# An S5, GLA and differential-attention trunk on one core: phase pieces of the first S5 layer, scaled sides of the second and attention's first split in another order

## The chip, the cores and the metric

The kernel runs on 1 core of one Trainium2 chip. The metric is device time in microseconds (us), the median of several executions. Engines: TensorE (PE) multiplies matrices, with its weight loads (PEld) beside it; VectorE (DVE) and ScalarE (ACT) work element by element; GpSimd (POOL) clears tiles and issues DMAs; SyncE (SP) issues most DMAs. Each engine works through its own instructions in order and waits on semaphores for the others.

## The reference

A batch of one, 512 positions, 1024 features, four layers: S5, gated linear attention (GLA), differential attention, S5. Each layer is a mixer and a SwiGLU network, each behind an RMS norm and added to its input. What matters here is the S5 mixer: 64 groups of 16 features have 64 complex states each, with a decay, a rotation per step, an input matrix and an output matrix:

```
p_ang = li * dt * j
p_re = p_mag * jnp.cos(p_ang)
p_im = p_mag * jnp.sin(p_ang)
...
y = jnp.einsum('bcgp,ghp->bcgh', s_re, cr) - jnp.einsum('bcgp,ghp->bcgh', s_im, ci)
...
y = y + d_skip.astype(f32) * h.astype(f32)
z = jax.nn.gelu(y).astype(h.dtype)
a, b = jnp.split(z @ w_glu, 2, axis=-1)
return a * jax.nn.sigmoid(b)
```

The attention projects to q, k and v, turns a quarter of each head by its position, and takes for each of 8 heads the difference of two softmaxes, `a = p[:, :, 0] - lam * p[:, :, 1]`, times v.

## The kernel before, in words

All is float32. A matrix product at full width is made of parts: each operand is split into a high part (a cast to the PE's float32 format) and a low part (the operand less its high part), and three products are added (`mm3`, L376, L377, L378). For weights the high part is cast by ACT (`high`, L348, tile whl) and the low part subtracted by DVE (`low_now`, L356); weights come through three staging tiles (wst) and lie in five whl tiles. PSUM has four banks for sums (acc), two for V (s) and two for turned tiles and small outputs (tp).

**An S5 layer** is a pipe over eight blocks of 128 features (`s5_pipe`, L1341). For block kk: its input is transposed (`up`, L1366, PE) and copied to a tile "room" by ACT (L1379), or in the second S5 layer for the first four blocks multiplied by the norm's factor on DVE (L1375, Rt); `products` gives V on PE (L1387); `states` turns V by cosines and sines on DVE (L1392 to L1397); two scans with the decays run along time on DVE (L1401); four `turn`s turn back on DVE (L1414, L1410) and leave prods; `outputs` adds y on PE (L1421 with the block's map from a DMA to scr, L1423 with prods) and takes its gelu on ACT (L1425); `turned` transposes it (zp, L1438, PE) and casts it to zT (L1439, ACT); `rest` subtracts its low part (L1443, DVE); `glu` multiplies two steps later with the gate's weights.

A step of the loop (ten of them) issues, in order: states(kk), outputs(kk-1), up(kk+2), turned(kk-1), products(kk+1), the scans and turns of kk, rest(kk-1), glu(kk-2). Between these stand hooks, named by their place ("behind states", "operators", "ahead of zp", "behind products", "behind scans", "beside"). In this pipe all five engines keep the order in which the code issues (`hand_all`): a step's place in the code is its place in each engine's row.

The first S5 layer has to make its cosines and sines itself, in the hooks. Each block has four pieces (`s5_phases_first`): **rough** (two products on PE, L1012 and L1013, then two roundings on ACT, L1014 and L1016, to tile turnsr), **angle** (three products on PE, L1020 to L1022, the second of which needs turnsr), **clip** (one DVE instruction, L1025, which reads the angle and writes cs), **sines** (three ACT instructions: Abs L1028, Sin L1029, Sin L1030). states of a block needs its sines. Beside these the hooks build, for every two blocks, the input matrices (X, L1052 to L1054 and L1077 on DVE; transposed as xps, L1188, PE; copied as inm, L1211, ACT), the output matrices (Q; transposed as cps, L1098, PE; copied, L1119, ACT; L1052 to L1054, DVE), and the map within a block: rps (L1154, PE), its two copies rsb (L1164, DVE; L1168, ACT), a DMA to memory (rd, L1170) and eight DMAs back to scr (L1179). The decays r are copied by ACT (L1038). Sin and gelu use different tables of ACT; where one follows the other an ACT_TABLE_LOAD stands between.

In the second S5 layer these matrices come from memory; its first four blocks are transposed ahead of the norm (`up_first`), and their multiply by Rt is what `up` issues in steps 0 and 1 for blocks 2 and 3.

**The attention** (L2090) fixes only PE's order by hand; the other engines' rows are set by a scheduler, which `issue_after` can bind to stand behind a given instruction. A projection is 32 units of three products, drawn by `run(units, n)`; the evacuation of a projection to q or k is L2152 (ACT), L2157 to L2163 (DVE), a transposition L2168 and a copy L2169 (ACT); that of v is L2174 (ACT). `prepare(j)` splits the queries and keys of head j: tile hl, high part on ACT (L2188), low part on DVE (L2189), then DMAs of POOL's queue to qs and ks. The code around the change:

```
units = project(0, 2)
run(units, 8)
rest()
prepare(0)
run(units)
```

Of the kernel before, what the change touches and what calls it, by code (L numbers as in the profile page):

```python
# [268 lines left out]
class Trunk:  # L269
# [1071 lines left out]
    def s5_pipe(self, L, hu, zT, natural, room, get, before=None, hooks=None, steps=None, left=None):  # L1341
# [114 lines left out]
        if hooks:  # L1456
            hook = lambda name, kk: hooks[name](kk) if name in hooks else None
            self.hand_all()
            if left:
                for kk in range(4):  # L1460
                    up_first(kk)
            before(up, products)
            for kk in range(10):
                if kk % 2 == 0 and kk:
                    hls[kk // 2 - 1] = self.high(stage[kk // 2 - 1], 2, 512)
                hook("first", kk)
                if kk < 8:
                    states(kk)
                if kk == 7:
                    rest(5)  # L1470
                if kk % 2 == 0 and kk:
                    self.low(hls[kk // 2 - 1], stage[kk // 2 - 1])
                hook("behind states", kk)
                if 1 <= kk < 9:
                    outputs(kk - 1)
                hook("operators", kk)
                if kk + 2 < 8:
                    up(kk + 2)
                hook("ahead of zp", kk)
                if 1 <= kk < 9:  # L1480
                    turned(kk - 1)
                if kk == 8:
                    glu(6)
                if kk + 1 < 8:
                    products(kk + 1)
                hook("behind products", kk)
                if kk < 8:
                    scan(kk, 0)
                    scan(kk, 1)
                    hook("behind scans", kk)  # L1490
                    for k in range(4):
                        turn(kk, k)
                hook("beside", kk)
                if 1 <= kk < 9 and kk != 6:
                    rest(kk - 1)
                if kk % 2 == 0 and kk < 8:
                    stage[kk // 2] = self.staged(self.wb_src(wg, kk, D), 2, 512)
                if kk >= 2 and kk != 8:
                    glu(kk - 2)
                hook("last", kk)  # L1500
            self.hand()
            return accs
# [33 lines left out]
    def s5_first(self, ctx):  # L1536
# [5 lines left out]
        with self.tc.tile_pool(name="s5_0", bufs=1) as p:  # L1542
# [92 lines left out]
                raw[2] = self.s5_loads(p, 0, 16, 8, 2)  # L1635

            def first(kk):
                if kk == 1:
                    phases((5, "angle"))
                if kk == 2:  # L1640
                    raw[3] = self.s5_loads(p, 0, 24, 8, 2)
                if 1 <= kk < 7:
                    decays(kk + 1)

            def behind_states(kk):
                if kk == 0:
                    phases((1, "clip"))
                    self.s5_map(0, 0, 8, rv[0], rs, mops[0])

            def operators(kk):  # L1650
                if kk in (2, 4, 6):
                    h = kk // 2
                    rv[h] = self.s5_rows(8, bp, Q[h][0])
                    if h > 1:
                        self.s5_map(0, 8 * h, 8, rv[h], rs, mops[h % 2])
                if 1 <= kk < 7:
                    ins(kk + 1)
# [5 lines left out]
            def behind_products(kk):  # L1663
                if kk == 0:
                    phases((3, "angle"), (4, "rough"))
                if kk == 1:
                    phases((6, "rough"), (7, "rough"), (6, "angle"))
                if kk == 2:
                    phases((7, "angle"))
                if kk == 3:  # L1670
                    phases((4, "sines"), (5, "sines"), (6, "sines"), (7, "sines"))
                if kk % 2 == 0 and 2 <= kk < 7:
                    out_pads(kk + 1)

            def behind_scans(kk):
                if kk == 0:
                    phases((2, "clip"), (2, "sines"), (4, "angle"), (5, "rough"))
                if kk == 1:
                    phases((4, "clip"), (5, "clip"))
                if kk == 2:  # L1680
                    self.s5_map(0, 8, 8, rv[1], rs, mops[1])
                    phases((6, "clip"))

            def beside(kk):
# [8 lines left out]
                    self.s5_b_pads(bp, X[h + 1][0])  # L1693
                if kk % 2 == 0 and kk < 6:
                    new_q(h + 1)
                if kk == 0:
                    phases((3, "clip"), (3, "sines"))
                if kk % 2 and kk < 7:
                    Q[h + 1][2]()
                    Q[h + 1][3]()  # L1700
                    out_pads(kk + 1)

            rv = {}
            hooks = {
                "first": first, "operators": operators, "behind states": behind_states, "ahead of zp": ahead_of_zp,
                "behind products": behind_products, "behind scans": behind_scans, "beside": beside,
            }
            accs = self.s5_pipe(0, hu, zT, True, room, get, before, hooks)
# [377 lines left out]
    def diff(self, l, left, after):  # L2086
# [4 lines left out]
        with self.tc.tile_pool(name="diff", bufs=1) as p:  # L2091
# [185 lines left out]
            units = project(0, 0)  # L2277
            run(units)
            tables()
            units = project(0, 1)  # L2280
            run(units)
            units = project(0, 2)
            run(units, 8)
            rest()
            prepare(0)
            run(units)

            def projections():
# [146 lines left out]
```

## Time and profile before

| what | us |
|---|---|
| median of three executions | 2316.88 |
| lowest, highest | 2314.95, 2317.75 |
| the profiled execution | 2316.13 |
| its span | 2314.4 |

A profile holds one execution. A row of the timeline gives the start, the length, engine, line, operation, what is written and read, the shape and, in brackets, how long the engine was idle ahead of it and who released it. Rows of one engine overlap a little: what an instruction costs its engine is the distance from its start to the next one's. A product on PE is a pipelined matmul, so its row is longer than that distance. A row of the waits adds such idle times by who waited for whom. A window gives the busy time of each engine in a stretch, and "PEclk", the share of full speed at which PE's clock ran there. The first S5 layer's pipe runs from about 38 to 165 us, the attention's first half to 1256, the second S5 layer's pipe from about 1804.

### The profile page before, as it was taken

Reading aid. Unit: us, or ns where it says so; the run is one execution under the profiler, and the core shown is the slowest. Engines: PE = TensorE matmul, PEld = TensorE weight load, DVE = VectorE, ACT = ScalarE, POOL = GpSimd, SP = SyncE. Lnnn points to the kernel's source line nnn. Section 1 sums busy time; section 2 is a strip of 40 time slices with the busy share of each in tenths; the row PEclk is TensorE's granted clock in tenths of the full one; section 3 lists DMA queues with packets and bytes.
Section 4 is the critical chain, followed back from the end, with each engine's and each line's share of the span. In section 5 each row is a group of like instructions: output and inputs, shape, how many; then the busy total and the mean of one; then the engine's idle time right before and its main releaser. Section 6 shows DMA issues by size and latency. Waiting matters only on the chain. (4 is left out here: it accounts for less than half of the span.)

```text
span 2314.4 us, 37179 instructions
## 1 busy us (share of the span) xinstructions
PE 2219.4 (96%) x14847; PEld 1970.1 (85%) x14847; DVE 1593.2 (69%) x2461; ACT 1108.2 (48%) x1769; POOL 284.6 (12%) x394
## 2 busy tenths in 40 slices
PE   5899999999999999999999999999999899999997
PEld 3788979898877799898988787899999788989996
DVE  8784977786624578777745675976766965957674
ACT  5533645454453355555535675654534224635342
POOL 1000140522000010100002131110000100101000
PEclk9999999999999999999999999999999899999999
DMA  4156567663422457665237365886641555766521
GB/s 86 39 146 172 131 173 183 164 179 100 124 71 73 137 140 190 170 177 164 92 124 156 90 152 136 223 210 146 163 103 46 140 153 150 201 157 162 159 80 64
DMA packets 293927, 319.91 MB, mean 138 GB/s; under 512 B 70077, under 2 KB 233177, under 8 KB 293498
## 3 DMA queue, kind: packets, MB, share of 16 engines
q1 hardware_dynamic: 231130, 235.79, 33.6%
q0 software_dynamic: 62624, 81.75, 18.9%
q8 instruction: 117, 1.92, 0.3%
q14 instruction: 56, 0.46, 0.1%
HBM read 285.62 MB, written 16.65 MB: 131 GB/s over the span
## 5 line engine op out<-in xcount | busy, mean ns | idle before, releaser
L356 DVE TENSOR_TENSOR whl<-wst,whl 128x1024 fp32r<-128x1024 f32 x272 | 331.1, 1222 | 264.5 <-ACT whl L348 263.4
L348 ACT CAST whl<-wst 128x1024 fp32r<-128x1024 f32 x272 | 284.3, 1050 | 336.9 <-PE acc L378 232.8
L543 PE MATMUL a<-side,whl 128*128 128x256 f32 x3168 | 382.4, 277 | 6.1 <-DVE whl L356 6.0
L543 PEld LDWEIGHTS a<-side,whl 128*128 128x128 f32 x3168 | 369.9, 188 | 7.8 <-DVE whl L356 6.7
L376 PE MATMUL acc<-whl,act 128*128 128x512 f32 x704 | 278.0, 395 | 2.6 <-DVE g L588 2.6
L377 PE MATMUL acc<-whl,act 128*128 128x512 f32 x704 | 274.9, 390 | 0.0
L378 PE MATMUL acc<-whl,act 128*128 128x512 f32 x704 | 274.7, 390 | 0.0
L543 PE MATMUL c<-side,whl 128*128 128x256 f32 x2112 | 256.2, 278 | 7.2 <-DVE whl L356 7.2
L543 PEld LDWEIGHTS c<-side,whl 128*128 128x128 f32 x2112 | 248.4, 189 | 8.2 <-DVE whl L356 8.2
L356 DVE TENSOR_TENSOR whl<-slot,whl 128x1024 fp32r<-128x1024 f32 x105 | 127.8, 1222 | 66.0 <-ACT whl L348 65.9
L376 PEld LDWEIGHTS acc<-whl,act 128*128 128x128 f32 x704 | 132.1, 188 | 31.9 <-DVE g L588 3.0
L378 PEld LDWEIGHTS acc<-whl,act 128*128 128x128 f32 x704 | 132.2, 188 | 27.9
L377 PEld LDWEIGHTS acc<-whl,act 128*128 128x128 f32 x704 | 132.2, 188 | 25.9 <-issue 0.2
L348 ACT CAST whl<-slot 128x1024 fp32r<-128x1024 f32 x105 | 110.0, 1053 | 74.0 <-PE acc L378 28.2
L376 PE MATMUL acc<-whl,hT 128*128 128x512 f32 x352 | 142.8, 406 | 2.1 <-DVE ro L2160 1.5
L377 PE MATMUL acc<-whl,hT 128*128 128x512 f32 x352 | 138.0, 392 | 0.9 <-DVE whl L356 0.9
L378 PE MATMUL acc<-whl,hT 128*128 128x512 f32 x352 | 138.1, 392 | 0.0
L543 PE MATMUL a<-sides,whl 128*128 128x256 f32 x1056 | 133.9, 283 | 1.2 <-DVE x L526 1.2
L543 PE MATMUL d<-sides,whl 128*128 128x256 f32 x1056 | 133.4, 282 | 1.3 <-ACT whl L348 1.3
L543 PEld LDWEIGHTS a<-sides,whl 128*128 128x128 f32 x1056 | 129.4, 191 | 2.3 <-issue 1.6
L543 PEld LDWEIGHTS d<-sides,whl 128*128 128x128 f32 x1056 | 128.8, 191 | 1.9 <-ACT whl L348 1.9
L680 ACT CAST act<-r 128x512 fp32r<-128x512 f32 (+1 forms) x110 | 66.2, 644 | 105.1 <-DVE r L661 86.1
(449 smaller groups left out, 3901.1 us busy)
## 6 DMA issues: line engine op xcount, KB each, us to landing
wst<-in_ffn_w_gate_up_dram SPq DMA_DIRECT2D x88, 512.0 KB, 4.5
wst<-in_ffn_w_down_dram SPq DMA_DIRECT2D x88, 512.0 KB, 4.4
slot<-in_ffn_w_gate_up_dram SPq DMA_DIRECT2D x69, 512.0 KB, 5.8
wst<-in_ffn_w_gate_up_dram POOLq DMA_DIRECT2D x44, 512.0 KB, 6.1
halves<-in_ffn_w_gate_up_dram SPq DMA_DIRECT2D x42, 512.0 KB, 5.5
wst<-in_s_w_glu_dram SPq DMA_DIRECT2D x32, 512.0 KB, 4.9
wst<-in_gla_w_in_dram SPq DMA_DIRECT2D x24, 512.0 KB, 3.6
wst<-in_diff_w_qkv_dram SPq DMA_DIRECT2D x24, 512.0 KB, 4.0
```

The costliest lines, as they stand in the source:

```text
L348: self.last["high"] = self.nc.scalar.copy(hl[:, 0], w[:])
L356: self.last["low"] = self.nc.vector.tensor_tensor(hl[:, 1], w[:], hl[:, 0].bitcast(F32), op=ALU.subtract)
L376: mm(out, lh, rh, start=first, stop=False)
L377: mm(out, lh, rl, start=False, stop=False)
L378: self.last["mm"] = mm(out, ll, rh, start=False, stop=last)
L543: mm(o, hl[:, x, k, c], side[:, y, k], start=first and not (j or k or n), stop=k == 3 and n == 2, skip_group_check=True,)
L680: self.last["act high"] = nc.scalar.copy(dst[:, 0, j], src[:, j])
```

## The change

Three edits, all of order; no instruction is added but two loads of ACT's tables.

First S5 layer: the angles of blocks 4 and 5 move from ahead of y(0) to the hook "operators" of step 1, behind y(0); those of blocks 6 and 7 to that of step 2, behind y(1). The clip and sines of block 3 move up behind states(1), the clips of blocks 4 and 5 down behind Q's DVE work in step 1. The sines of blocks 4 to 7, so far one row of twelve ACT instructions in step 3, go to a new hook "behind zp": blocks 4 and 5 in step 3, blocks 6 and 7 in step 4.

Second S5 layer: the multiplies of blocks 2 and 3 by Rt are issued behind the turns of steps 0 and 1 instead of ahead of V.

Attention: nine more units of the value projection are issued ahead of prepare(0), which is bound behind the last weight split issued by then.

```diff
--- before.py
+++ after.py
@@ -1474,11 +1474,13 @@
                 if 1 <= kk < 9:
                     outputs(kk - 1)
                 hook("operators", kk)
-                if kk + 2 < 8:
+                late = left and kk + 2 < 4
+                if kk + 2 < 8 and not late:
                     up(kk + 2)
                 hook("ahead of zp", kk)
                 if 1 <= kk < 9:
                     turned(kk - 1)
+                hook("behind zp", kk)
                 if kk == 8:
                     glu(6)
                 if kk + 1 < 8:
@@ -1490,6 +1492,8 @@
                     hook("behind scans", kk)
                     for k in range(4):
                         turn(kk, k)
+                if late:
+                    up(kk + 2)
                 hook("beside", kk)
                 if 1 <= kk < 9 and kk != 6:
                     rest(kk - 1)
@@ -1635,8 +1639,6 @@
                 raw[2] = self.s5_loads(p, 0, 16, 8, 2)
 
             def first(kk):
-                if kk == 1:
-                    phases((5, "angle"))
                 if kk == 2:
                     raw[3] = self.s5_loads(p, 0, 24, 8, 2)
                 if 1 <= kk < 7:
@@ -1646,8 +1648,14 @@
                 if kk == 0:
                     phases((1, "clip"))
                     self.s5_map(0, 0, 8, rv[0], rs, mops[0])
+                if kk == 1:
+                    phases((3, "clip"), (3, "sines"))
 
             def operators(kk):
+                if kk == 1:
+                    phases((4, "angle"), (5, "angle"))
+                if kk == 2:
+                    phases((6, "angle"), (7, "angle"))
                 if kk in (2, 4, 6):
                     h = kk // 2
                     rv[h] = self.s5_rows(8, bp, Q[h][0])
@@ -1664,19 +1672,17 @@
                 if kk == 0:
                     phases((3, "angle"), (4, "rough"))
                 if kk == 1:
-                    phases((6, "rough"), (7, "rough"), (6, "angle"))
-                if kk == 2:
-                    phases((7, "angle"))
-                if kk == 3:
-                    phases((4, "sines"), (5, "sines"), (6, "sines"), (7, "sines"))
+                    phases((6, "rough"), (7, "rough"))
                 if kk % 2 == 0 and 2 <= kk < 7:
                     out_pads(kk + 1)
 
+            def behind_zp(kk):
+                if kk in (3, 4):
+                    phases((2 * kk - 2, "sines"), (2 * kk - 1, "sines"))
+
             def behind_scans(kk):
                 if kk == 0:
-                    phases((2, "clip"), (2, "sines"), (4, "angle"), (5, "rough"))
-                if kk == 1:
-                    phases((4, "clip"), (5, "clip"))
+                    phases((2, "clip"), (2, "sines"), (5, "rough"))
                 if kk == 2:
                     self.s5_map(0, 8, 8, rv[1], rs, mops[1])
                     phases((6, "clip"))
@@ -1693,16 +1699,16 @@
                     self.s5_b_pads(bp, X[h + 1][0])
                 if kk % 2 == 0 and kk < 6:
                     new_q(h + 1)
-                if kk == 0:
-                    phases((3, "clip"), (3, "sines"))
                 if kk % 2 and kk < 7:
                     Q[h + 1][2]()
                     Q[h + 1][3]()
                     out_pads(kk + 1)
+                if kk == 1:
+                    phases((4, "clip"), (5, "clip"))
 
             rv = {}
             hooks = {
-                "first": first, "operators": operators, "behind states": behind_states, "ahead of zp": ahead_of_zp,
+                "first": first, "operators": operators, "behind states": behind_states, "ahead of zp": ahead_of_zp, "behind zp": behind_zp,
                 "behind products": behind_products, "behind scans": behind_scans, "beside": beside,
             }
             accs = self.s5_pipe(0, hu, zT, True, room, get, before, hooks)
@@ -2282,7 +2288,9 @@
             units = project(0, 2)
             run(units, 8)
             rest()
-            prepare(0)
+            run(units, 9)
+            with self.tc.issue_after(self.last["high"].ins), self.tc.issue_after(self.last["low"].ins):
+                prepare(0)
             run(units)
 
             def projections():
```

PE in the first S5 layer, around y(0) (the rows L1421 and L1423) and ahead of it (- before, + changed; "angle" is a block's three products, cps the transposition for Q, xps the one for inm):

```order
 L1013 MATMUL rough<-counts,frow 128x512
-L1020 MATMUL angle<-counts,frow 128x512
-L1021 MATMUL angle<-turnsr,nident 128x512
-L1022 MATMUL angle<-counts,frow 128x512
 L1012 MATMUL rough<-counts,frow 128x512
 L1013 MATMUL rough<-counts,frow 128x512
 L1098 MATMUL cps<-ident,craw 64x128 x8
-L1020 MATMUL angle<-counts,frow 128x512
-L1021 MATMUL angle<-turnsr,nident 128x512
-L1022 MATMUL angle<-counts,frow 128x512
 L1421 MATMUL y<-scr_97,room_348 128x128
 L1423 MATMUL y<-scr_97,prods 128x128 x4
```

The six angle products of blocks 4 and 5 now stand behind y(0), ahead of xps. In the same way those of blocks 6 and 7 stand behind y(1), ahead of rps, where block 6's stood ahead of y(1) and block 7's behind V(3).

ACT in the first S5 layer, steps 3 and 4 (cs are the sines' tiles, z and gain the gelu's, Q the copies of cps):

```order
-L1028 ACTIVATE cs_351<-cs_351 128x512
-L1029 ACTIVATE cs_351<-cs_351 128x512
-L1030 ACTIVATE cs_351<-cs_351,halfpi 128x512
-L1028 ACTIVATE cs_351<-cs_351 128x512
-L1029 ACTIVATE cs_351<-cs_351 128x512
-L1030 ACTIVATE cs_351<-cs_351,halfpi 128x512
-L348 CAST whl<-wst 128x1024
-L1038 COPY r_1035<-s5r_127 128x512
+L348 CAST whl<-wst 128x1024
+L1038 COPY r_1029<-s5r_127 128x512
 L1425 ACT_TABLE_LOAD
 L1425 ACTIVATE z_349<-y 128x8x4x16
```

```order
 L1439 CAST zT<-zp 128x4x128
+L1028 ACTIVATE cs_351<-cs_351 128x512
+L1029 ACT_TABLE_LOAD
+L1029 ACTIVATE cs_351<-cs_351 128x512
+L1030 ACTIVATE cs_351<-cs_351,halfpi 128x512
+L1028 ACTIVATE cs_351<-cs_351 128x512
+L1029 ACTIVATE cs_351<-cs_351 128x512
+L1030 ACTIVATE cs_351<-cs_351,halfpi 128x512
 L1119 ACTIVATE Q<-cps 64x8x16 x4
 L1038 COPY r_1199<-s5r_127 128x512
+L1425 ACT_TABLE_LOAD
 L1425 ACTIVATE gain<-y 128x8x4x16
```

Two blocks' sines leave the place ahead of gelu(3) and stand, with a load of Sin's table ahead and one of gelu's behind, between zT(3) and gelu(4), ahead of the Q copies.

ACT in the attention, around the first split (hl), first before, then changed (qtm and qk are a projection's evacuation, vall the values'):

```order
L2152 ACTIVATE qtm<-acc,rcol 128x512 x4
L348 CAST whl<-wst 128x1024
L2169 COPY qk<-qTp 128x4x128 x4
L2152 ACTIVATE qtm<-acc,rcol 128x512 x4
L2169 COPY qk<-qTp 128x4x128 x4
L2188 CAST hl<-qk 128x1024
L348 CAST whl<-wst 128x1024 x5
L2188 CAST hl<-qk 128x1024 x2
L2174 ACTIVATE vall<-acc,rcol 128x512 x4
```

```order
L2158 ACTIVATE qtm<-acc,rcol 128x512 x4
L348 CAST whl<-wst 128x1024
L2175 COPY qk<-qTp 128x4x128 x4
L348 CAST whl<-wst 128x1024 x2
L2158 ACTIVATE qtm<-acc,rcol 128x512 x4
L2175 COPY qk<-qTp 128x4x128 x4
L2194 CAST hl<-qk 128x1024
L348 CAST whl<-wst 128x1024 x3
L2194 CAST hl<-qk 128x1024 x2
L2180 ACTIVATE vall<-acc,rcol 128x512 x4
```

Two of the five weight casts behind hl now stand ahead of the last qtm copies; DVE's two subtractions move likewise. The order of PE is unchanged there, and so are the rows of POOL and SP everywhere.

## The prediction

> **What bounds the kernel now.** The page comes first: which engine fills the span.
>
> ```profile
> PE 2219.4 (96%) x14847; PEld 1970.1 (85%) x14847; DVE 1593.2 (69%) x2461; ACT 1108.2 (48%) x1769; POOL 284.6 (12%) x394
> ```
>
> TensorE (PE) is busy in 2219.4 of 2314.4 us, so at most 95 us are idle, and an edit that computes nothing less can only close idle time or make PE run faster. The three edits lie in three short stretches, so each is read there: waits, timeline, windows. The first S5 layer (38 to 165 us) comes first. VectorE's (DVE's) waits in its first half are "engine, line, for whom: total, times, longest":
>
> ```profile
> DVE cs L1025 <- PE angle L1022: 5.8, 3, 4.1
> DVE zT L1443 <- ACT zT L1439: 3.9, 1, 3.9
> DVE rsb L1164 <- PE rps L1154: 2.2, 1, 2.2
> DVE whl L356 <- ACT whl L348: 0.4, 1, 0.4
> ```
>
> These 12.3 us are DVE's idle time from 50 to 88. The windows show what comes behind, and the clock (columns: stretch, length, then busy and count of PE, PEld, DVE, ACT, POOL; PEclk, DMA share, GB/s):
>
> ```profile
> 56.00:59.40 3.40, 3.40 (x14) 1.76 (x11) 2.26 (x4) 2.82 (x8) 0.00 (x0) 0.50 0.02 5
> 73.10:76.40 3.30, 3.30 (x15) 3.06 (x16) 2.90 (x5) 2.18 (x3) 0.11 (x1) 0.53 0.02 5
> 88.00:155.00 67.00, 58.95 (x583) 52.76 (x581) 66.52 (x110) 30.46 (x51) 6.69 (x16) 0.97 0.31 69
> ```
>
> From 88 to 155 DVE works 66.52 of 67.00 us. What it gains before 88 it can keep, and nothing but DVE limits it there. The first two rows show PE at half clock around y(0) and y(1), with PE wholly busy.
>
> **First S5, the path of PE.** The timeline of PE (start, length, then the instruction, and the idle time before it):
>
> ```profile
> 50.45 0.39 PE L1012 MATMUL rough<-counts,frow 12*128 12x512 f32 x1
> 50.92 0.38 PE L1020 MATMUL angle<-counts,frow 12*128 12x512 f32 x1
> ...
> 56.63 0.79 PE L1020 MATMUL angle<-counts,frow 12*128 12x512 f32 x1
> 58.80 0.80 PE L1421 MATMUL y<-scr,room 128*128 128x128 f32 x2
> ...
> 65.49 1.15 PE L1188 MATMUL xps<-ident,X 64*64 64x64 f32 x32
> ...
> 71.32 0.38 PE L1020 MATMUL angle<-counts,frow 12*128 12x512 f32 x1
> ...
> 73.39 0.80 PE L1421 MATMUL y<-scr,room 128*128 128x128 f32 x2
> ...
> 79.64 0.69 PE L1154 MATMUL rps<-Q,bpad 128*32 128x64 f32 x32
> ...
> 86.52 0.50 PE L1020 MATMUL angle<-counts,frow 12*128 12x512 f32 x1
> ...
> 87.81 1.09 PE L1098 MATMUL cps<-ident,craw 128*64 128x128 f32 x16
> ...
> 92.58 0.46 PE L1421 MATMUL y<-scr,room 128*128 128x128 f32 x2 [0.71 <-DMA scr<-rd]
> ...
> 97.21 1.15 PE L1188 MATMUL xps<-ident,X 64*64 64x64 f32 x32
> ...
> 109.23 0.69 PE L1154 MATMUL rps<-Q,bpad 128*32 128x64 f32 x32
> 113.23 1.15 PE L1188 MATMUL xps<-ident,X 64*64 64x64 f32 x32 [3.31 <-ACT z L1425]
> ```
>
> Prices: an angle product is 1.29 warm (86.52 to 87.81) and 2.17 cold (56.63 to 58.80); y is 4.63 warm (92.58 to 97.21), while y(0) took 6.69 and y(1) 6.25. A rough product takes 0.47 (50.45 to 50.92).
>
> Angles 4 and 5 leave the way to y(0), with angle 4's wait for its turns. Behind rough(4) (to 50.92) stand rough(5), 0.47, and the C transposes (cps), 1.09 warm: y(0) may start at 52.5 instead of 58.80. It also needs block 0's map, whose last DMAs are these:
>
> ```profile
> 47.12 2.35 POOL L1179 DMA_DIRECT2D scr<-rd  x4 [2.12 <-DMA rd<-rsb]
> ...
> scr<-rd POOLq DMA_DIRECT2D x4, 32.0 KB, 2.1
> ```
>
> Issued by 49.5 and landing 2.1 later, the map is there at 51.6. y(0)'s length isn't shown by any row, since the clock may be either; between 4.63 and 6.69 I take the middle, 5.66, because the angles' small products, which filled the time right ahead of y(0) and waited there, leave, while V and the roughs stay. So y(0) ends at 58.1, angles 4 and 5 (2 x 1.29) at 60.7, and xps(2) starts there: 4.8 ahead. ScalarE (ACT) now has sines(3) behind states(1) and a table load behind them, ahead of gelu(0); if these come late, the angles' 2.6 on PE cover them.
>
> Angle 6 leaves the stretch ahead of y(1): 71.32 to 73.39, 2.07, its wait included. y(1) I take as warm, 1.62 less. Angles 6 and 7 now stand ahead of rps, 2.58 more. Lead of PE at rps: 4.8 + 2.1 + 1.6 - 2.6 = **5.9**. Angle 7's 1.29 behind V(3) goes too, but y(2) waits for map 1 (its row, 0.71), whose chain starts at rps, so the lead there stays 5.9.
>
> **First S5, DVE.** clip(7) stood behind a 4.12 wait (the longest above) for an angle that now comes before rps: DVE's blocks behind it come 5.9 + 4.1 = 10.0 earlier. Then two things are late next:
>
> ```profile
> 107.64 0.67 DVE L1392 TENSOR_TENSOR mods<-V,cs 128x512 f32<-128x512 f32 x1
> ...
> 112.37 0.35 DVE L1164 SCALAR_TENSOR_TENSOR rsb<-mask,dcol,rps 128x16 f32<-128x16 f32 x2
> ```
>
> ```profile
> 101.89 1.28 ACT L1029 ACT_TABLE_LOAD   x1
> 103.18 0.63 ACT L1029 ACTIVATE cs<-cs 128x512 f32<-128x512 f32 x1
> ...
> 104.33 0.61 ACT L1028 ACTIVATE cs<-cs 128x512 f32<-128x512 f32 x1
> ...
> 106.13 0.61 ACT L1028 ACTIVATE cs<-cs 128x512 f32<-128x512 f32 x1
> ...
> 116.81 1.10 ACT L1439 CAST zT<-zp 128x512 fp32r<-128x512 f32 x1 [0.59 <-PE zp L1438]
> 120.14 1.14 ACT L1119 ACTIVATE Q<-cps 64x128 f32<-64x128 f32 x4 [2.22 <-PE cps L1098]
> 122.88 0.39 PE L1421 MATMUL y<-scr,room 128*128 128x128 f32 x2
> ```
>
> states(4) (107.64) would start at 97.6, but block 4's sines end at 104.33 - 5.9 = 98.4: 0.8 waited. rsb stands 4.73 behind, at 103.2, but rps of step 4 ends at 109.92 - 5.9 = 104.0: 0.8 more. From there DVE's lead is 112.4 - 104.0 = **8.3**, and it works without a gap to 155.
>
> PE must not lose it. The 3.31 ahead of xps(5) was gelu(3) behind four blocks of sines; with two blocks fewer (3.6) that wait goes, and PE leads by 9.2. The moved pair, sines 6 and 7, now stands ahead of the Q copies: 2 x 1.80 (104.33 to 106.13) and one table load, 1.28: 4.9 behind zT(3), which ends at 117.9 on the old time. Q is copied by 123.9 on that time, and y(4), which takes cps's bank, was due at 122.88: PE waits 1.0 there and leads by **8.2**. The second load, ahead of gelu(4), falls into ACT's idle time during y(4). I take 8.2 for this layer.
>
> On the clock, the Trainium skill (TensorE: Matmul & The Clock Gate, Part 1) says that PE is halved after an idle window of about 3.4 us and restored after a busy one. The trace disagrees with the first half: 56.00 to 59.40 is 3.40 of 3.40 busy at 0.50. By that rule a PE which never idles for so long stays warm; that is a rival below.
>
> On the table loads a page speaks against this change: the Trainium skill (ScalarE: Activation LUTs, What ACT_TABLE_LOAD costs) gives each switch 1.28 us and about 1.38 of draining, and its rules ask to finish one set before switching. In the row at 103.18 Sin starts right behind the load, so I see no drain. By the page, estimated, PE would wait 2.4 at y(4) instead of 1.0.
>
> Bounds of this layer: all warm, L = 6.9, ends 1.0 better, 9.2. All cold (cps at 1.98, both y as they were, each pair of angles 4.34): y(0) starts at 53.4, xps(2) at 64.4, a lead of 1.1; plus 2.07 less 4.34 leaves PE 1.2 late at rps, and DVE gains 112.4 - 111.1 = 1.3.
>
> **Attention's first split.** Rows of PE, ACT and DVE around block 0's preparation:
>
> ```profile
> 1226.34 0.51 PE L376 MATMUL acc<-whl,hT 128*128 128x512 f32 x1 [0.61 <-ACT whl L348]
> 1227.79 0.50 PE L377 MATMUL acc<-whl,hT 128*128 128x512 f32 x1 [0.95 <-DVE whl L356]
> ```
>
> ```profile
> 1216.45 2.73 ACT L2152 ACTIVATE qtm<-acc,rcol 128x512 f32<-128x512 f32 x4 [15.83 <-PE acc L378]
> ...
> 1240.96 2.00 ACT L2188 CAST hl<-qk 128x1024 fp32r<-128x1024 f32 x2 [2.30 <-DMA ks<-hl]
> ```
>
> PE waits 1.56 for a weight tile whose cast and subtraction stand behind hl. Both splits now stand ahead of the qtm copies, in 15.83 of idle ACT time, so the 1.56 goes: **1.5**. What may be late instead is hl, and with it the DMAs to qs and ks; the hl casts of the next blocks wait for those already (2.30), ahead of the value copies. That can give 0.5 back; so 1.0 to 1.6.
>
> **Second S5.**
>
> ```profile
> 1808.17 0.68 DVE L1375 TENSOR_TENSOR room<-up,Rt 128x512 f32<-128x512 f32 x1
> 1808.77 2.33 DVE L1401 TENSOR_TENSOR_SCAN mods<-cs,mods 128x512 f32<-128x512 f32 x2
> ...
> 1811.74 2.59 PE L1423 MATMUL y<-out,prods 128*128 128x128 f32 x8 [3.10 <-DVE prods L1414]
> ```
>
> The multiply takes 0.60 (1808.17 to 1808.77) ahead of the scan for which y(0) waits 3.10. Behind the turns it delays only states(1), one step ahead of its reader. Gain 0 to 0.6; the half clock in that y(0) (2.59 for eight products, 1.06 warm would do) ends at its own time, so I take **0.5**.
>
> **Sum:** 8.2 + 1.5 + 0.5 = 10.2. The profiled execution took 2316.13, of which 2314.4 is the span; that gives 2305.9, and its distance to the median of 2316.88, 0.75, gives **2306.7**.
>
> **The rivals.** A change under 0.2%, 4.6 us, can't be told from none.
>
> *Forecast*, 0.54: S5 7 to 9.2.
>
> *Colder y blocks*, 0.19: y(0) and y(1) stay half cold, angles warm. L = 5.9 - 1.0 - 1.6 = 3.3, S5 5.6, sum 7.6: 2309.3. For it: 73.10 to 76.40 is at 0.53 although V and the roughs, which stay, filled the time before.
>
> *Never cold*, 0.08: all products warm, S5 9.2, sum 11.2: 2305.7. The row at 56.00 speaks against it. It is what the Trainium skill's clock rule gives.
>
> *Dear loads*, 0.03: a switch takes twice its row, PE waits 2.3 at y(4), S5 6.9, sum 8.9: 2308.0. The Sin at 103.18 speaks against it. It is what the Trainium skill's drain would do.
>
> *Given back*, 0.11: DVE and PE reach the glu products early and wait there for weights, or all is cold (1.3 + 1.5 + 0.5 = 3.3): 2313.6 to 2314.9, no change. Against the first: DMA share is 0.31 from 88 to 155.
>
> *Slower*, 0.05: map 0 lands late, since the pads' DMAs and a weight tile share its queues, and y(0) waits for it. With y(0) at its old 58.80 and 6.69 long, the cold pair behind it (4.34) makes xps(2) 4.3 late; 2.07 is won ahead of y(1), the second pair costs 4.34 again: rps 6.6 late. In step 4 rps ends at 109.92 + 6.6 = 116.5, and DVE is 4.1 late, PE, with the Q copies' 1.0, 4.3; less the other edits' 2.0 that is 2.3 slower. It decides from y(0) at 56.5, a landing of 7.0 behind the last issue against 2.1 in the row; a landing of 12 makes it 5.0 slower, 2321.9.
>
> Faster by more than 0.2%: 0.54 + 0.19 + 0.08 + 0.03 = 0.84; same 0.12, slower 0.04, since the mildest of the slower case is no change. Range: low end between all warm (2305.7) and the ceiling with all of DVE's 12.3 gone (2316.88 - 14.3 = 2302.6), 2303.7; high end between the colder case (2309.3) and all cold (2313.6), 2312.0.
>
> **What would show it.** Right: y(0) starts near 52.5, xps(2) near 60.7, rps of step 2 near 73.8; no wait of clip(7); states(4) and rsb wait under 1 us each; PE waits about 1 us ahead of y(4); S5's last y block starts 8 earlier; no wait at L376 and L377 near 1216; the second S5's y wait 2.5. Wrong: clock rows at 0.5 in both y blocks and both pairs, a wait of 3 or more at y(4), or a lead that is there at 112 and gone at 165.

## The result, and the profile after

| | before | changed |
|---|---|---|
| median of four runs, us | 2317.32 (2314.95 to 2319.80) | 2305.05 (2303.92 to 2306.58) |
| ratio | 1 | 0.9949, 95% interval 0.9936 to 0.9962 |
| profiled execution, us | 2316.13 | 2303.92 |
| its span; mean granted clock | 2314.4; 0.989 | 2302.2; 0.991 |

The change takes 12.3 us off, 0.5%. The forecast was 2306.7. From the page of the changed kernel, the busy times:

```profile
PE 2211.6 (96%) x14847; PEld 1963.9 (85%) x14847; DVE 1593.8 (69%) x2461; ACT 1110.8 (48%) x1771; POOL 284.6 (12%) x394
```

PE runs the same 14847 products in 7.8 us less busy time (2219.4 before). No product was removed; PE's clock was higher during part of the time. ACT has two instructions more, the second pair of table loads.

PE's timeline in the first S5 layer, changed kernel (start, length, instruction, and in brackets the idle time ahead of it):

```profile
48.84 0.39 PE L1012 MATMUL rough<-counts,frow 12*128 12x512 f32 x1
...
50.88 0.49 PE L1421 MATMUL y<-scr,room 128*128 128x128 f32 x2
...
55.55 0.50 PE L1020 MATMUL angle<-counts,frow 12*128 12x512 f32 x1
...
57.91 1.15 PE L1188 MATMUL xps<-ident,X 64*64 64x64 f32 x32
...
64.05 0.49 PE L1421 MATMUL y<-scr,room 128*128 128x128 f32 x2
...
68.71 0.50 PE L1020 MATMUL angle<-counts,frow 12*128 12x512 f32 x1
...
71.08 0.69 PE L1154 MATMUL rps<-Q,bpad 128*32 128x64 f32 x32
...
86.03 0.77 PE L1421 MATMUL y<-scr,room 128*128 128x128 f32 x2 [4.15 <-DMA scr<-rd]
...
93.61 1.15 PE L1188 MATMUL xps<-ident,X 64*64 64x64 f32 x32
...
106.41 1.15 PE L1188 MATMUL xps<-ident,X 64*64 64x64 f32 x32
...
117.45 0.49 PE L1421 MATMUL y<-scr,room 128*128 128x128 f32 x2 [2.22 <-DVE zT L1443]
```

```profile
151.21 0.39 PE L1421 MATMUL y<-scr,room 128*128 128x128 f32 x2
```

Read it against the rows of before in steps. y(0) takes 4.67 (50.88 to 55.55) where it took 6.69, and y(1) 4.66 where it took 6.25: both are warm now, that is, at full clock. rps of step 2 is at 71.08 instead of 79.64, 8.6 ahead. Of that, 1.6 was there before anything had moved: rough(4) stands at 48.84 instead of 50.45 (a second profile of the kernel before has it at 49.35, so it is no effect of the change). Then y(2) gives back much of it. It waits 4.15 for map 1's DMAs instead of 0.71, and then takes 7.58 (86.03 to 93.61) instead of 4.63, cold after that wait. xps(5) at 106.41 has no wait (3.31 before). The last y block starts at 151.21 instead of 157.20: 6.0 ahead, 4.4 without the 1.6.

The clock, from the changed kernel's windows (stretch, length; busy and count of PE, PEld, DVE, ACT, POOL; PEclk, DMA share, GB/s):

```profile
56.00:59.40 3.40, 3.06 (x38) 1.83 (x37) 3.37 (x6) 3.34 (x6) 0.00 (x0) 1.00 0.00 0
...
73.10:76.50 3.40, 1.70 (x13) 1.47 (x14) 3.33 (x7) 1.90 (x4) 0.00 (x0) 1.00 0.00 0
```

The stretch that ran at 0.50 runs at 1.00. The counts, 38 against 14, don't compare: by now 32 of the 38 are the short products of xps. DVE's waits from 48 to 88, changed kernel ("for whom: total, times, longest"):

```profile
DVE rsb L1164 <- PE rps L1154: 1.0, 1, 1.0
DVE zT L1443 <- ACT zT L1439: 0.8, 1, 0.8
DVE whl L356 <- ACT whl L348: 0.4, 1, 0.4
```

2.2 us are left of 12.3; clip's wait for an angle, 5.8, is gone. The next two waits came where the forecast looked for them, the first at 1.88 instead of 0.8 (DVE's timeline):

```profile
100.84 0.69 DVE L1392 TENSOR_TENSOR mods<-V,cs 128x512 f32<-128x512 f32 x1 [1.88 <-ACT cs L1030]
...
106.44 0.37 DVE L1164 SCALAR_TENSOR_TENSOR rsb<-mask,dcol,rps 128x16 f32<-128x16 f32 x2 [0.79 <-PE rps L1154]
```

In the attention, no row of PE between 1200 and 1235 has a wait any more; the two of L376 and L377 (1.56 together) are gone. In the second S5 the y wait is shorter (3.10 before):

```profile
1799.17 2.59 PE L1423 MATMUL y<-out,prods 128*128 128x128 f32 x8 [2.41 <-DVE prods L1414]
```

### The profile page after: what moved, and what is told of

Same layout as the page of the kernel before. It is cut to its first block, busy times and chain, and to the rows that moved or that the text cites. A ratio compares the mean times of both kernels' runs of the same rounds, so it can differ in the third digit from the quotient of the medians.

```text
span 2302.2 us, 37175 instructions
## 1 busy us (share of the span) xinstructions
PE 2211.6 (96%) x14847; PEld 1963.9 (85%) x14847; DVE 1593.8 (69%) x2461; ACT 1110.8 (48%) x1771; POOL 284.6 (12%) x394
## 5 line engine op out<-in xcount | busy, mean ns | idle before, releaser
L376 PE MATMUL acc<-whl,act 128*128 128x512 f32 x704 | 278.7, 396 | 0.7 <-DVE g L588 0.7
L377 PE MATMUL acc<-whl,act 128*128 128x512 f32 x704 | 275.4, 391 | 0.0
L376 PEld LDWEIGHTS acc<-whl,act 128*128 128x128 f32 x704 | 132.5, 188 | 30.2 <-DVE g L588 1.1
L377 PEld LDWEIGHTS acc<-whl,act 128*128 128x128 f32 x704 | 132.7, 188 | 26.2 <-issue 0.2
L348 ACT CAST whl<-slot 128x1024 fp32r<-128x1024 f32 x105 | 110.0, 1052 | 73.8 <-PE acc L378 27.9
L376 PE MATMUL acc<-whl,hT 128*128 128x512 f32 x352 | 142.7, 405 | 1.0 <-DVE ro L2166 1.0
L377 PE MATMUL acc<-whl,hT 128*128 128x512 f32 x352 | 137.8, 392 | 0.0
```

The source lines that it names most:

```text
L348: self.last["high"] = self.nc.scalar.copy(hl[:, 0], w[:])
L376: mm(out, lh, rh, start=first, stop=False)
L377: mm(out, lh, rl, start=False, stop=False)
```

## The experiments

**The two kernels again.** No edit. This shows what one profile of each is worth.

> The kernel before, unchanged, for a second profile. Theory A (the clock's windows fall at random): V(0), y(0), y(1) change their lengths against the first profile (V(0) 3.78, y(0) 6.69, y(1) 6.25) and the last y block of the first S5 layer starts up to 3 us off 157.20. Theory B (the clock follows the work): the same rows come out within 0.2 us.

> The changed kernel, unchanged, for a second profile and a narrower ratio. Theory A (random windows): the 4.15 wait of y(2) for its map stays, since the map's chain starts behind zT(1), but y(2)'s length moves between 4.6 and 7.6, and V(0) between 2.05 and 3.8. Theory B: the map's late landing (9.0 us behind its copy against 6.9 before) was a chance of that run; the wait falls to about 2. Time against before 0.993 to 0.997.

The changed kernel has a median of 2306.36 of five runs, ratio 0.9946 (0.9931 to 0.9960). Its profile repeats the late map: y(2) waits 3.45 and is cold; y(7) starts at 150.60. The kernel before gave 2315.38 in its one run, beside a median of 2317.07. There y(0) and y(1) are cold again: from a block's first to its last product with room, 57.60 to 63.19 is 5.6 and 72.31 to 77.39 is 5.1, against 3.5 in the changed kernel. y(7) starts at 156.12, 1.1 earlier than in the first profile, but rough(4) is 1.1 earlier too: from there on the two take the same time.

**The three edits one by one.** Edit 1 is the first S5's order, edit 2 the second S5's multiply, edit 3 the attention's split. Each kernel holds one edit alone:

```diff
 # s5_first: the changed kernel, with
-                late = left and kk + 2 < 4
+                late = False
...
-            run(units, 9)
-            with self.tc.issue_after(self.last["high"].ins), self.tc.issue_after(self.last["low"].ins):
-                prepare(0)
+            prepare(0)
```

> Only the first S5 layer's edit. By the prediction's sum 8.2 us less, about 0.9965 of before. By the two profiles only 4.4 of the 6.0 us by which the layer ended earlier come from the moved work, 0.998; the rest, 1.6, was there at V(1) already, ahead of anything moved.

```diff
 # att: the kernel before, with
-            prepare(0)
+            run(units, 9)
+            with self.tc.issue_after(self.last["high"].ins), self.tc.issue_after(self.last["low"].ins):
+                prepare(0)
```

> Only the attention's edit. By the prediction's sum 1.5 us less (the two waits of PE in the value projection). By the two profiles 3.6: 2.1 at the first score product, and 1.5 more near the fourth head's split, whose wait for the DMAs of the keys fell from 4.05 to 2.55. The rival: the second 1.5 is no effect of this edit and won't be there.

```diff
 # s5_second: the kernel before, with
-                if kk + 2 < 8:
+                late = left and kk + 2 < 4
+                if kk + 2 < 8 and not late:
...
+                if late:
+                    up(kk + 2)
```

> Only the second S5 layer's edit: y(0)'s wait for its products falls from 3.1 to 2.5, and the last step of that layer starts 0.3 to 0.6 earlier against its first states. The rival: 1.3 us, what the first two profiles show from the layer's start to its end.

| kernel | median, us (runs) | ratio (95% interval) | y(7) of the first S5 starts |
|---|---|---|---|
| s5_first | 2309.40 (6) | 0.9960 (0.9945 to 0.9975) | 149.48 |
| att | 2313.85 (12) | 0.9981 (0.9971 to 0.9991) | 160.21 |
| s5_second | 2315.58 (10) | 0.9996 (0.9986 to 1.0006) | 161.88 |

Edit 1 is worth 9.3 us by its ratio, edit 3 4.4, edit 2 0.9, which can't be told from nothing. The sum, 14.6, is more than the whole's 12.3, but each interval is 2.3 to 3.5 us wide on either side. The column at the right shows a second thing: kernels with the same old order in the first S5 reach y(7) anywhere from 156.1 to 161.9, so a forecast made from one profile had a base that moves by 5. The two late ones, att and s5_second, have a longer cold stretch: y(1) takes 7.5 there and V(3) 3.3, against 6.25 and 1.95 (the profile of s5_second is also the slowest of its ten runs, 2320.18).

In s5_first the map isn't late, and y(2) is warm. PE's rows there:

```profile
85.80 0.46 PE L1421 MATMUL y<-scr,room 128*128 128x128 f32 x2 [0.84 <-DMA scr<-rd]
...
90.43 1.15 PE L1188 MATMUL xps<-ident,X 64*64 64x64 f32 x32
```

It takes 4.63, and the lead over the kernel before goes from 7.0 at rps (72.62 against 79.64) to 6.8 behind y(2) (90.43 against 97.21) and 7.7 at y(7).

The attention's edit is worth more than the 1.56 of waits. Head 0's first score comes 2.1 earlier, against the shift just ahead of it: idle time in these rows is counted from the end of the row before, 0.39 to 0.40 long, while products start 0.23 apart, and a product after a wait has a row of 0.50. The rest is farther on. ACT's hl cast of head 3 and the product that waits behind it, in the kernel before, and then the casts in the changed one:

```profile
1274.46 1.05 ACT L2188 CAST hl<-qk 128x1024 fp32r<-128x1024 f32 x1 [4.05 <-DMA ks<-hl]
...
1276.05 1.16 PE L2246 MATMUL op<-vall,aT 128*128 128x128 f32 x8 [0.75 <-ACT aT L2238]
```

```profile
1230.52 1.05 ACT L2194 CAST hl<-qk 128x1024 fp32r<-128x1024 f32 x1 [4.38 <-PE acc L378]
...
1264.73 1.05 ACT L2194 CAST hl<-qk 128x1024 fp32r<-128x1024 f32 x1 [2.55 <-DMA ks<-hl]
```

In the kernel before, the hl casts of heads 1 and 2 came together at 1240.96, behind a wait for the DMAs to ks. Now the first of them is at 1230.52. Head 3's cast then waits 2.55 for those DMAs instead of 4.05, and PE's wait of 0.75 at its next output products is 0. The shorter wait holds in all fourteen profiles, those further down included: it is 3.70 to 4.89 in the seven without edit 3 and 1.99 to 3.01 in the seven with it.

**The two halves of edit 1.** One kernel keeps the new places of clips and angles and leaves all sines ahead of gelu(3); the other only divides the sines:

```diff
 # angles: edit 1 with
             def behind_zp(kk):
-                if kk in (3, 4):
-                    phases((2 * kk - 2, "sines"), (2 * kk - 1, "sines"))
+                pass
...
+                if kk == 3:
+                    phases((4, "sines"), (5, "sines"), (6, "sines"), (7, "sines"))
```

> The first S5 layer's edit without the division of the sines: the angles and clips are moved, the sines of blocks 4 to 7 stay one row of twelve in step 3. By the prediction's sum the angles carry the gain and the division only takes away gelu(3)'s wait: xps(5) again waits about 3 us for gelu(3), y(4) no longer waits 2.2 for its bank, DVE's waits stay as in the run with the whole edit; the layer ends within 1.5 us of that run (149.4 to 151). The rival: the division carries half of it, and the layer ends 3 or more later, at 152.5 or above.

```diff
 # sines: the kernel before, with
+                hook("behind zp", kk)
...
-                if kk == 3:
-                    phases((4, "sines"), (5, "sines"), (6, "sines"), (7, "sines"))
...
+            def behind_zp(kk):
+                if kk in (3, 4):
+                    phases((2 * kk - 2, "sines"), (2 * kk - 1, "sines"))
...
```

> The division of the sines alone, angles and clips where they were. DVE has no wait from 88 on in the kernel before, so nothing is expected of it: xps(5)'s wait of 3.31 goes, a wait at y(4) comes, the layer ends within 1 us of before (156.2 to 157.2). The rival (PE's own waits count): the 3.31 is worth 1 to 3 us.

angles: 2312.70, 0.9978 (0.9967 to 0.9990), y(7) at 154.16. sines: 2317.15, 1.0005 (0.9995 to 1.0015), y(7) at 157.27. PE and DVE in angles, then PE in sines:

```profile
87.25 0.77 PE L1421 MATMUL y<-scr,room 128*128 128x128 f32 x2 [3.70 <-DMA scr<-rd]
...
110.81 1.98 PE L1188 MATMUL xps<-ident,X 64*64 64x64 f32 x32 [3.26 <-ACT z L1425]
```

```profile
108.36 1.22 DVE L356 TENSOR_TENSOR whl<-wst,whl 128x1024 fp32r<-128x1024 f32 x1 [2.63 <-ACT whl L348]
```

```profile
113.25 0.66 PE L1366 MATMUL up<-ident,scr 128*128 128x128 f32 x4 [1.66 <-ACT rsb L1168]
...
123.51 0.49 PE L1421 MATMUL y<-scr,room 128*128 128x128 f32 x2 [1.14 <-DVE zT L1443]
```

Division alone removes the 3.31 and earns nothing. In its place come 1.66 for ACT's rsb copy and 1.14 for DVE's rest(3): behind xps DVE is just as late. In angles DVE does come earlier and then waits 2.63 for a weight's cast, which stands behind the twelve sines on ACT; in s5_first and in the changed kernel that wait is gone. So the forecast for angles, 149.4 to 151, failed. What the division is worth there isn't settled: from 0.9978 to 0.9960 is about 4 us, but the two intervals overlap, and in its profile angles also has the late map and a cold y(2) (7.58), which s5_first hasn't. Against the changed kernel, which has both too, y(7) is 1.3 later, both taken from rough(4).

**Map 1 earlier.** In the changed kernel the chain from rps to y(2) got longer. ACT and SP there, before and then changed:

```profile
85.70 0.30 ACT L1168 COPY rsb<-rps 128x96 f32<-128x96 f32 x1
86.03 0.37 SPq L1170 DMA_DIRECT2D rd<-rsb  x1
87.86 2.89 SPq L1179 DMA_DIRECT2D scr<-rd  x4
```

```profile
77.02 0.31 ACT L1168 COPY rsb<-rps 128x96 f32<-128x96 f32 x1
77.36 0.37 SPq L1170 DMA_DIRECT2D rd<-rsb  x1
81.32 1.76 SPq L1179 DMA_DIRECT2D scr<-rd  x4
```

From the issue of rd<-rsb to the first issue that needs it, 1.83 before and 3.96 after; from the copy to y(2), 6.9 and 9.0. The experiment puts ACT's copy right behind the gelu at which rps is done, so that the chain starts earlier:

```diff
 # map_early: the changed kernel, with
-        nc.scalar.copy(rs[:, :nk, 64:112], rv[:, :nk, 16:64])
+        if not copied:
+            nc.scalar.copy(rs[:, :nk, 64:112], rv[:, :nk, 16:64])
...
+                    if h == 1:
+                        nc.scalar.copy(rs[:, :2, 64:112], rv[h][:, :2, 16:64])
...
-                    self.s5_map(0, 8, 8, rv[1], rs, mops[1])
+                    self.s5_map(0, 8, 8, rv[1], rs, mops[1], copied=True)
```

> The changed kernel, with ACT's copy of the second map (rsb) moved from behind zT(1) to behind gelu(1), so that the map's DMAs start about 5 us sooner. If the late map is what gives the gain back, y(2) no longer waits (4.15 and 3.45 in the two profiles), DVE's wait for zT(2) (3.9 and 1.8) and part of its 1.9 for the sines go, and the layer ends 2 to 5 earlier than 151.2 and 150.6: time 0.5 to 2 permille under the changed kernel. The rival: PE's early y(2) only waits later (at y(4), whose bank comes with rest(3)), and nothing is won.

2299.37, ratio 0.9927 (0.9911 to 0.9943). y(2) starts without a wait, 5.4 before the changed kernel's, and is warm; y(7) starts at 144.71 instead of 151.21, 6.5 earlier, where 2 to 5 was expected:

```profile
80.59 0.46 PE L1422 MATMUL y<-scr,room 128*128 128x128 f32 x2
```

So what the changed kernel gives back at y(2) is map 1's lateness and the cold block behind it. Not all of it is the earlier copy: the DMA rd<-rsb was also back at 1.83 here, and why is open (below).

**What makes PE cold: rows or waits.** The rough products and two of a block's three angle products use 12 of the array's 128 rows (12*128 in the profile), and the angles also wait for turns. Either could have made the clock drop. The windows of before, 3.41 long, around the drop ahead of V(1), the one ahead of y(0), and the clock's return:

```profile
42.33:45.74 3.41, 2.89 (x13) 1.39 (x11) 3.33 (x6) 2.54 (x5) 0.11 (x1) 1.00 0.00 0
45.74:49.15 3.41, 3.41 (x18) 3.19 (x17) 3.41 (x7) 3.17 (x5) 2.04 (x4) 0.54 0.32 75
49.15:52.56 3.41, 2.15 (x7) 1.11 (x6) 2.86 (x6) 1.41 (x3) 0.32 (x1) 0.96 0.57 77
52.57:55.98 3.41, 3.37 (x16) 2.27 (x18) 3.41 (x5) 2.87 (x5) 0.00 (x0) 0.54 0.53 156
...
59.39:62.80 3.41, 3.41 (x18) 3.41 (x17) 3.41 (x7) 2.21 (x3) 0.11 (x1) 0.50 0.00 0
62.80:66.22 3.42, 3.42 (x47) 3.30 (x48) 2.97 (x5) 0.60 (x1) 0.00 (x0) 0.96 0.00 0
```

A window that is 2.89 busy, most of it rough and angle products, is followed by one at 0.54, and so is one that is 2.15 busy. From there the clock stays down through wholly busy windows and comes back behind 59.39 to 62.80, which y(0)'s products of 128 rows fill. The test pads both operands to 128 rows with zeros, which adds nothing to the sums and leaves the order and the causes of the waits as they are:

```diff
 # rows128: the kernel before, with
-        self.frow = cp.tile([12, 8, P], F32R, name="frow")
+        self.frow = cp.tile([P, 8, P], F32R, name="frow")
+        for k in range(8):
+            nc.gpsimd.tensor_scalar_mul(self.frow[:, k], self.ident[:], 0.0)
...
-        self.counts = cp.tile([12, 2, 4, P], F32R, name="counts")
+        self.counts = cp.tile([P, 2, 4, P], F32R, name="counts")
...
```

> The kernel before, with the two operands of the rough and angle products (frow, counts) padded by zeros from 12 rows to 128; results and order stay. All profiles of the old order have y(0) and y(1) at half clock (5.1 to 6.5 from their first to their last row, 3.5 warm), those of the new order have both warm. Theory A: PE's clock follows how many rows of the array work, and stretches full of 12-row products count as idle. Then with 128 rows y(0) and y(1) come out warm in the old order too, 3.5 each, and the layer ends 2 to 5 earlier than 157.2. Theory B: it follows the time in which PE waits. The waits stay (1.3, 0.5, 0.8), so y(0) and y(1) stay at 5.1 to 6.5, and the time stays within 1 us.

2303.97, ratio 0.9949 (0.9935 to 0.9962): with the old order, the whole gain of the change. Two windows of this kernel, then PE's rows:

```profile
45.74:49.15 3.41, 1.93 (x19) 1.41 (x20) 3.38 (x7) 3.35 (x7) 0.83 (x2) 1.00 0.58 85
49.15:52.56 3.41, 2.91 (x25) 2.33 (x22) 3.41 (x6) 3.27 (x8) 0.00 (x0) 1.00 0.64 162
```

```profile
47.31 0.50 PE L1023 MATMUL angle<-turnsr,nident 128*128 128x512 f32 x1 [1.48 <-ACT turnsr L1018]
...
51.02 0.38 PE L1423 MATMUL y<-scr,room 128*128 128x128 f32 x2
...
55.57 1.15 PE L1190 MATMUL xps<-ident,X 64*64 64x64 f32 x32
```

The waits for turns are still there, 3.7 in all against 2.7 before, and one window has only 1.93 of products in it; yet the clock stays at 1.00 and y(0) takes 4.55. V(1), y(0) and y(1) are warm in all four profiles with padding, the three below included. That refutes the waits as the cause; it is the few rows. How the clock's control counts them isn't shown. The Trainium skill (TensorE: Matmul & The Clock Gate, Part 1) halves the clock after an idle window of about 3.4 us. With padded products the trace agrees (1.93 busy is not idle), and it agrees at y(2), cold after 3.45 and 4.15 of waiting and warm after 0.84; with 12-row products it differs, since the clock fell behind windows that were 2.89 and 2.15 busy. y(7) starts at 144.57, 12.6 earlier than before, where 2 to 5 was expected. Not all of that is the clock: a group of three angle products takes 0.77 here (44.20 to 44.97), where it takes 1.29 unpadded even when warm.

**Padding with the new order, and all together.** Three kernels: padding on the changed kernel; padding and the early copy on it; and these two with the first S5's old order but edits 2 and 3.

```diff
 # after_rows128 = changed + rows128's edit
 # map_rows128 = changed + rows128's edit + map_early's edit
 # old_rows128_map = map_rows128 with the first S5's hooks as before:
-            def behind_zp(kk):
-                if kk in (3, 4):
-                    phases((2 * kk - 2, "sines"), (2 * kk - 1, "sines"))
...
+                    phases((6, "rough"), (7, "rough"), (6, "angle"))
```

> The changed kernel with the padding to 128 rows. If the first S5 layer's new order won by keeping 12-row products away from the y blocks (clock), the padding has taken that gain already: the layer ends within 2 us of the padded old order (y(7) at 144.7), and the time is about 0.998 of it, the attention's and second layer's 3 to 5 us; against before 0.992 to 0.994. If it won by taking waits and products from DVE's way, its 5 to 8 us come on top: y(7) near 138, ratio 0.990.

> The changed kernel with the early map copy, and the padding on top. Theory A: what is still cold in the S5 layer there (V(1) 3.36, V(5) 3.0) gets shorter where rough and angle products stand ahead (V(1)), at most 1.7 earlier. Theory B: no change against the early map copy alone, ratio 0.992 to 0.994.

> The old order of the first S5 layer with the padding and the early map copy, and the change's other two edits. If the order of the angles matters little once the clock holds, this comes out with the same time as the changed order with padding and early map copy (ratio 0.9915), y(7) within 1.5 us of 141.7; if the order still matters, 3 us or more slower.

| kernel | median, us (runs) | ratio (95% interval) | y(7) starts |
|---|---|---|---|
| after_rows128 | 2299.66 (6) | 0.9921 (0.9904 to 0.9939) | 145.01 |
| map_rows128 | 2296.96 (4) | 0.9915 (0.9902 to 0.9929) | 141.52 |
| old_rows128_map | 2297.47 (6) | 0.9914 (0.9899 to 0.9928) | 143.44 |

With padding, y(7) starts no earlier in the new order (145.01) than in the old (144.57); with the map early too, 1.9 earlier, and the totals are equal. The distance from rows128 to after_rows128, 4.3 us by the medians and 6.5 by the ratios, is about what edits 2 and 3 are worth (5.3 above). In map_rows128 V(1) is warm, as theory A has it, and y(7) is 3.2 earlier than in map_early, more than the 1.7 expected. Both versions with padding and the early copy beat both kernels by a clear margin, the best being 2296.96. after_rows128 still has the late map:

```profile
80.20 0.77 PE L1423 MATMUL y<-scr,room 128*128 128x128 f32 x2 [3.54 <-DMA scr<-rd]
```

So padding doesn't warm a block that PE enters after 3.5 us without any products.

## Why the prediction was right, and where its steps were off

The total (2306.7 against 2305.05) was right, and up to rps of step 2 its chain is the one that the traces show. That the sum fits so closely is in part luck. Between the two profiled executions, 12.2 us apart, the changed kernel is ahead by 1.6 at rough(4), where nothing had moved yet, by 6.0 at y(7), by 8.2 behind the attention's two waits (1219.89 against 1228.12), by 9.7 at head 3 (1269.65 against 1279.38) and by 12.2 in the second S5 layer (1851.78 against 1863.99). So in this pair the first S5 layer gave 4.4 where 8.2 was forecast, and what lies behind it 6.2 where 2.0 was. Point by point, with starts of the changed kernel moved by the 1.61 that its rough(4) came earlier:

- **y(0)'s start.** Forecast 52.5; 50.88 + 1.61 = 52.49.
- **Length of y(0).** The step "between 4.63 and 6.69 I take the middle, 5.66" was off: 4.67. y(1) as warm was right. So xps(2) is at 59.5 (forecast 60.7) and rps at 72.7 (forecast 73.8): 1.1 more lead.
- **"The lead there stays 5.9".** This step failed. The map's chain was taken at its old length, 6.9 from copy to y(2); it took 9.0, and y(2), which the prediction never considered cold, lost another 2.95. Of 7.0 of lead 2.0 are left at xps behind y(2) (97.21 less 93.61, less 1.61). In s5_first, where the chain takes 6.8, 6.8 are left.
- **DVE's lead.** Forecast 8.3 at rsb, made of PE's 5.9 and of the 2.4 by which DVE had been late there. The working holds with other numbers: in s5_first rsb is at 103.26, 9.1 ahead, with waits of 1.12 (states(4)) and 0.77 (rsb) where 0.8 each was forecast; in the changed kernel the waits are 1.88 and 0.79, and 112.37 less 106.44, less 1.61, is 4.3.
- **y(4).** "PE waits 1.0 there" for the Q copies named the wrong releaser. It waits 2.2 for rest(3), since from here DVE and not ACT is last, in the changed kernel, its repetition and s5_first alike. By the prediction's own argument, that DVE sets the pace from here, this costs nothing beyond DVE's lead.
- **The size of S5, 8.2.** By y(7) the means are 158.5 for five profiles of the old order and 150.4 for three of the new with the whole edit: 8.1, of which 1.1 is the earlier rough(4), so 7.0. Against the base profile alone and net of the start it is 4.4 and 4.9 where the map is late (the changed kernel and its repetition) and 7.7 where it isn't (s5_first). The mean came out near partly by luck: the base profile (157.2) was one of the better ones of the old order, and the loss at y(2) was not foreseen, two errors of opposite sign.
- **The division of the sines** was forecast to remove 3.31 from PE, with DVE's lead as the real limit. That limit is what sines shows: alone it earns nothing.
- **Attention, 1.5.** Mis-sized: 2.1 at the waits themselves, and 0.9 to 1.5 later at head 3, which "what may be late instead is hl" had with the wrong sign. att measures 4.4 with an interval of 2.3 on either side.
- **Second S5, 0.5.** The wait is 2.78 to 3.18 in the unpadded profiles without the edit and 2.41 to 2.59 in those with it, as forecast; with padding it is 2.06 without the edit and 1.16 to 2.59 with it. The term's 0.5 can't be resolved in the time.

The rivals. *Never cold* was right for y(0), y(1) and the angles of blocks 4 to 7, wrong for V(1) (3.78) and y(2); *Colder y blocks* was wrong. *Slower* needed map 0 to land late, and it didn't: y(0) has no wait. A late map did come, the other one. *Given back* didn't happen as named, at the glu products: of the 6.0 at y(7) 5.6 are left there (162.88 against 168.52), and the loss at y(2) is one that it doesn't name. *Dear loads* was wrong; ACT in the changed kernel around the new loads:

```profile
111.09 1.28 ACT L1029 ACT_TABLE_LOAD   x1
112.38 0.63 ACT L1029 ACTIVATE cs<-cs 128x512 f32<-128x512 f32 x1
...
117.11 1.28 ACT L1425 ACT_TABLE_LOAD   x1
```

Sin starts where the load's 1.28 ends, and the second load, as forecast, falls in idle time, 3.8 ahead of its gelu. The drain that the Trainium skill (ScalarE: Activation LUTs, What ACT_TABLE_LOAD costs) gives each switch doesn't show.

**Left open.** Why the DMA rd<-rsb, of 112 KB, takes 3.4 to 4.0 us to release the next one in four profiles (changed 3.96, its repetition 3.42, angles 3.57, after_rows128 3.36) and 1.8 to 2.0 in ten others. In all four a packet of the instruction queue of 0.02 MB was in flight with it; but in rows128 one was too, and the DMA took 1.83. No run shows what the instruction packet does.

## What to carry to other kernels

Before reordering work around a cold stretch of TensorE, look at how many rows its products use: here zeros in the unused rows of the old order gave as much as the whole change. When an edit brings one engine ahead, price the DMA chains that the gained lead runs into, and the clock behind the wait there: a map 2.1 us later took 5.0 of the 7.0 won. And take a stage's base from several profiles when its old state depends on the clock, since this one moved by 5 us with the same order of PE.

## What the hardware showed that was not expected

- A window filled to 2.89 of 3.41 us, mostly with 12-row products, was followed by one at clock 0.54, and a wholly busy one (56.00 to 59.40) stayed at 0.50; with the same products at 128 rows, 1.93 of 3.41 was enough for 1.00.
- A group of three angle products with 12, 128 and 12 rows starts its parts 0.42 to 0.44 apart at clock 1.00; with 128 rows throughout, also at 1.00, 0.23 to 0.31. Before, then padded:

```profile
86.94 0.50 PE L1021 MATMUL angle<-turnsr,nident 128*128 128x512 f32 x1
87.38 0.50 PE L1022 MATMUL angle<-counts,frow 12*128 12x512 f32 x1
```

```profile
74.57 0.39 PE L1023 MATMUL angle<-turnsr,nident 128*128 128x512 f32 x1
74.80 0.40 PE L1024 MATMUL angle<-counts,frow 128*128 128x512 f32 x1
```

- A wait of PE costs more than its idle time in the profile: 1.56 of waits, 2.1 of lead.
- The recorded clock can be wrong early in a profile: before shows 1.00 from 15 to 35 us, though xps takes 1.97 at 29.04, against 1.15 when warm. So a window's clock is read together with the lengths of its rows.
